# A hybrid encoder step on one core: a fixed order for the first loads and products, and regrouped outputs of state space and sample attention

## The chip, the core and the metric

The kernel runs on one core of a Trainium2 chip. The metric is device microseconds of one execution. Before the change the median of 3 runs is 2015.0 us (2014.14 to 2017.74). Engines are named as in the profile: PE is TensorE's products, PEld its weight loads, DVE VectorE, ACT ScalarE, POOL GpSimd, SP SyncE, which issues all DMAs of this kernel.

## The reference, cut to what matters

One layer works on a prompt of 1024 tokens and on 32 sample tokens with a past of 2048, all in float32, width 2048. The input is normalised, scaled and shifted by a modulation of the condition vector, and projected; four head groups read the projection, and a common output projection follows.

```python
shift, scale, gate = jnp.split(c @ w_mod + b_mod, 3, axis=-1)
u = layer_norm(x) * (1.0 + scale[:, None]) + shift[:, None]
(z_a, xbc_a, dt_a, q_b, k_b, v_b, g_b, x_c, ...) = split_cols(u @ w_in)
# A, state space, per chunk with carried state h:
y = jnp.einsum('bthn,bshn,btsh,bshp->bthp', cc, bc, decay, xdt)
y = y + jnp.einsum('bthn,bhpn,bth->bthp', cc, h, jnp.exp(acum))
# B, stick-breaking attention, swept over key blocks:
z = jnp.einsum('bqhd,bkhd->bhqk', qblk, k) * scale
out = jnp.einsum('bhqk,bkhd->bqhd', w, v)
```

## The kernel before, in words

The prompt is worked in two halves (h = 0 and 1, 512 tokens each); the 32 sample tokens ride with half 0, so that a row of that half has 544 columns. A column tile is 128 columns of w_in: `col_tile` (L336) loads its two halves of 512 KB, splits each into a high and a low part (ScalarE cast L326, VectorE subtraction L327), and adds three products for each of the 16 blocks k of 128 rows (wh*uh, wh*ul, wl*uh, L351 to L353), in half 0 over two spans of 272 columns: 96 products. The normalised and scaled input u is kept in the same two parts, `uh` and `ul`. The scale is applied when u is built (`build_u0`, L280: five transposes, two ScalarE activations, two VectorE instructions). The shift stands in two extra columns of u (`shift_columns`, L275), which the tiles with `shift` multiply along; the four gate tiles T_G do without.

The modulation comes from `mod_group(g, part)` (L205), for four groups of 512 columns and two parts (1 is the scale, 0 the shift): 16 loads of 256 KB each, and four times a quad of products, 32 columns of weights each on four strips of the array; then the sum is copied out (L227), turned with four small products (L229) and added to scale or shift. At the start the program traces the loads and norms of x (L1358), then the four groups of part 1 with the builds of u between them (L1361 to L1365), then the four gate tiles woven with part 0 (L1436).

The order of instructions on each engine is not that of the program: a planner places them by priority (`high_priority`) and by when it takes them to be ready. `behind(a, b)` (L197) puts one instruction behind another on its engine. Buffers come from pools: `io` has 20, of which five hold parts of x until u is built; `wr` has 2, `wh` and `wl` 3 each; the PSUM pool `ip` has 3, `z` 2, `s` 2, `a` 1.

The state-space unit `a_unit` (L528) runs 5 chunks (4 in half 1) for each of two groups of four heads. `weights` (L556) prepares a chunk; its matrix L has an exponential on ScalarE (L584) and a product with the mask on POOL (L585). `outputs` (L589), one step later, multiplies L with x*dt for each head (L597), C with the state (L600), combines both on VectorE (L605, L607), and updates the state (L609 to L614). `turn` (L621), another step later, transposes the result (L624) and adds the skip term (L626). A float32 product is two records in the trace.

The sample attention `b_sample` (L871) takes two pairs of heads at a time. For each of five key blocks it makes the scores of four heads with two products against a weight tile that is zero outside its heads (L917, `qb` from L784 to L788), and the values with eight products of 128 weight columns and 64 moving columns (L896).

`weave` (L1408) interleaves units in given numbers of steps.

Of the kernel before, what the change touches and what calls it, by code (L numbers as in the profile page):

```python
# [62 lines left out]
def step_kernel(ctx, tc, xp, xs, cst, wmss, wmg, bgate, win, wsm, wout, lng, lnb, ck, cv,  # L63
# [140 lines left out]

    def mod_group(g, part):  # L205
        o = ZT("mod")

        for kq in range(4):
            ws = []
            for i in range(4):  # L210
                wr = IO("wmr")
                nc.sync.dma_start(wr[:, 0:512], wmss[g, 4 * kq + i, part])
                ws.append(wr)
                if i < 3:
                    yield 1

            with tc.high_priority():
                after = None
                for i in (3, 0, 1, 2):
                    c0 = 2 * (4 * kq + i)  # L220
                    mm = T.matmul(o[32 * i:32 * i + 32], cpad[:, c0:c0 + 32], ws[i][:, 0:512], start=(kq == 0),  # L221
                                  stop=(kq == 3), skip_group_check=True)
                    after = behind(mm, after)
            yield 1
        pc = ST("modc")
        mr = WK("mr")
        V.tensor_copy(mr[:, 0:512], o)  # L227
        for j in range(4):
            T.matmul(pc[:, 2 * j:2 * j + 2], mr[:, j * P:(j + 1) * P], sel2c, start=True, stop=True)  # L229
# [13 lines left out]
    def load_norm(src, rows, keep):  # L243

        tiles = []
        for q in range(4):
# [4 lines left out]
            nc.sync.dma_start(t[:rows, 0:512], src[:, q * 512:(q + 1) * 512])  # L251
# [28 lines left out]
    def build_u0(xts, k):  # L280
# [5 lines left out]
        for t in range(4):  # L286
            T.transpose(pt[:, t * P:(t + 1) * P], xts[t][0][q][:, o * P:(o + 1) * P], ident)
        pt2 = AT("xt2")
        T.transpose(pt2[:, 0:SMP], xts[4][0][q][0:SMP, o * P:(o + 1) * P], ident[0:SMP, 0:SMP])
# [3 lines left out]
        V.tensor_tensor(ul[:, 2:546], uf[:, 0:544], uh[:, 2:546].bitcast(F32), op=ALU.subtract)  # L293
# [90 lines left out]
    def narrow(h):  # L384
# [95 lines left out]
        for c in range(nch):  # L480
# [11 lines left out]
            A.activation(col[0:n, c, 24:32], col[0:n, c, 0:8], AF.Exp)  # L492
# [35 lines left out]
    def a_unit(h, g):  # L528
# [27 lines left out]
        def weights(c, n, cc):  # L556
# [30 lines left out]
            return L, xd, bt, el  # L587

        def outputs(c, n, cc, L, xd, bt, el):  # L589
# [11 lines left out]
            y = WK("ya", [P, 2, 256])  # L601
            if first:
                V.tensor_copy(y[0:n, 0, :], py[0:n, 0:256])
            else:
                V.tensor_tensor(g4(y[0:n, 1, :], 4), g4(py[0:n, 256:512], 4),  # L605
                                col[0:n, c, 24 + 4 * g:28 + 4 * g].to_broadcast([n, 4, 64]), op=ALU.mult)
                V.tensor_tensor(y[0:n, 0, :], y[0:n, 1, :], py[0:n, 0:256], op=ALU.add)  # L607
# [11 lines left out]
            return y  # L619

        def turn(n, cc, y):  # L621
            pt = ST("pyt")
            for j in range(2):
                T.transpose(pt[:, j * P:j * P + n], y[0:n, 0, j * P:(j + 1) * P], ident[0:n, 0:n])  # L624
            for j in range(2):
                V.scalar_tensor_tensor(yg[j][:, cc], tiles[f"x{j}"][:, cc], C("dsk", 2 * g + j),  # L626
                                       pt[:, j * P:j * P + n], op0=ALU.mult, op1=ALU.add)

        todo1 = todo2 = None
        for c in range(nch + 2):  # L630
            done = todo2
            todo2 = None
            if todo1:
                todo2 = (*todo1[1:3], outputs(*todo1))
                todo1 = None
            if c < nch:
# [3 lines left out]
                todo1 = (c, n, cc, *weights(c, n, cc))  # L640
            if done:
                turn(*done)
# [91 lines left out]
    def b_gate(p):  # L734

        res = yield from col_tile(0, T_G + p, False)
        t = WK("graw")
# [4 lines left out]
        yield 2  # L742

    def b_unit(h, p):
# [26 lines left out]
        if h == 0:  # L771
# [8 lines left out]

# [3 lines left out]
            qb = sp.tile([P, P], F32, tag="qb", name=nm("qb"), bufs=2)  # L784
            G.memset(qb, 0.0)
            o = (p % 2) * 64
            G.tensor_copy(qb[0:64, o:o + 32], q[0:64, 512:544])
            G.tensor_copy(qb[64:128, o + 32:o + 64], q[64:128, 512:544])  # L788
# [82 lines left out]
    def b_sample(gq):  # L871
# [13 lines left out]
        def back(blk, w, vc):  # L885
# [7 lines left out]
            for b in range(nb):  # L893
                for j in range(2):
                    lhs = prs[j][2] if blk == 4 else vc[j][:, b * P:(b + 1) * P]
                    T.matmul(pa[:, 64 * j:64 * j + 64], lhs, wt[0:kn, b * P + 64 * j:b * P + 64 * j + 64],  # L896
                             start=(blk == 4 and j == 0), stop=(blk == 0 and b == nb - 1), skip_group_check=True)

        todo = None
        for blk in (4, 3, 2, 1, 0):  # L900
# [14 lines left out]
            for j in range(2):  # L915
                rhs = prs[j][1] if blk == 4 else kc[j][:, 0:512]
                T.matmul(z[:, 0:n], prs[j][0], rhs, start=(j == 0), stop=(j == 1))  # L917
# [6 lines left out]
        for j in range(2):  # L924
            ys = sp.tile([P, SMP], F32, tag="ysb", name=nm("ysb"))
            for hh in range(2):
                r = slice(64 * hh, 64 * hh + 64)
# [635 lines left out]
```

## Time and profile before

| | |
|---|---|
| median of 3 runs | 2015.0 us (2014.14 to 2017.74) |
| profiled execution | 2011.09 us, span 2009.2 us, clock 0.989 |
| TensorE busy | 1916.5 us, 95% |
| VectorE busy | 1341.6 us, 67% |
| ScalarE busy | 767.0 us, 38% |
| GpSimd busy | 272.7 us, 14% |
| HBM read, written | 253.49 MB, 35.82 MB |

The span is the time from the first to the last instruction of the profiled execution. Busy times are records laid over each other; matmuls overlap, so the pace of TensorE is read from one start to the next.

### The profile page before, as it was taken

The page shows a single profiled execution, that of the slowest core. Times are in us where ns is not written, and L with a number is a line of the kernel's source. Part 1 is how long each engine was busy: PE and PEld are TensorE (multiplying, and loading weights), DVE is VectorE, ACT ScalarE, POOL GpSimd, SP SyncE. Part 2 cuts the span into 40 slices and gives each one's busy share as a digit, 9 for nine tenths or more (in the row PEclk, how much of TensorE's full clock was granted, in tenths as well). Part 3 has the DMA queues.
Part 4 walks back from the last instruction along what each step waited for, and adds up shares of the span by engine and source line. Part 5 has one row for each costly group of instructions (what it writes and reads, how often), then busy time and mean ns, then how long its engine had stood idle before and what let it go on. Part 6 is the DMA issues. An engine that isn't in the chain of part 4 may idle for free. (4 is left out here: it accounts for less than half of the span.)

```text
span 2009.2 us, 31503 instructions
## 1 busy us (share of the span) xinstructions
PE 1916.5 (95%) x11956; PEld 1599.0 (80%) x11956; DVE 1341.6 (67%) x2610; ACT 767.0 (38%) x1278; POOL 272.7 (14%) x481
## 2 busy tenths in 40 slices
PE   3999999999999999999999999999999999998998
PEld 1578999998889999977787886777878676676787
DVE  4325667877956857876678779876857664355765
ACT  5212533334464434435444444533334421133321
POOL 1000111202211202331101011121111210000000
PEclk9999999999999999999999999999999999999998
DMA  9786344333443343644232332433433635457733
GB/s 320 260 282 226 119 127 127 118 121 121 138 145 119 105 117 101 175 126 139 91 113 94 113 101 85 122 99 102 126 99 101 210 107 184 151 190 239 226 128 131
DMA packets 162031, 291.38 MB, mean 145 GB/s; under 512 B 23836, under 2 KB 66076, under 8 KB 161880
## 3 DMA queue, kind: packets, MB, share of 16 engines
q1 hardware_dynamic: 161880, 289.37, 45.3%
q8 instruction: 94, 1.54, 0.3%
q14 instruction: 57, 0.47, 0.1%
HBM read 253.49 MB, written 35.82 MB: 144 GB/s over the span
## 5 line engine op out<-in xcount | busy, mean ns | idle before, releaser
L351 PE MATMUL ip<-uh,wh 128*128 128x272 f32 (+4 forms) x2368 | 775.8, 328 | 0.4 <-POOL uh L277 0.4
L352 PE MATMUL ip<-ul,wh 128*128 128x272 f32 (+4 forms) x2368 | 765.6, 323 | 0.0
L353 PE MATMUL ip<-uh,wl 128*128 128x272 f32 (+4 forms) x2368 | 764.1, 323 | 0.0
L326 ACT CAST wh<-wr 128x1024 fp32r<-128x1024 f32 (+1 forms) x257 | 268.3, 1044 | 671.2 <-PE ip L352 404.8
L327 DVE TENSOR_TENSOR wl<-wr,wh 128x1024 fp32r<-128x1024 f32 (+1 forms) x257 | 314.6, 1225 | 253.8 <-ACT wh L326 239.4
L351 PEld LDWEIGHTS ip<-uh,wh 128*128 128x128 f32 x2368 | 449.5, 190 | 38.9 <-issue 7.7
L352 PEld LDWEIGHTS ip<-ul,wh 128*128 128x128 f32 x2368 | 449.4, 190 | 37.7 <-issue 7.0
L353 PEld LDWEIGHTS ip<-uh,wl 128*128 128x128 f32 x2368 | 449.3, 190 | 37.7 <-issue 7.3
L1241 PE MATMUL op<-wh,yh 128*128 128x512 f32 (+1 forms) x576 | 215.9, 375 | 7.6 <-DVE val L1252 7.6
L1243 PE MATMUL op<-wh,yl 128*128 128x512 f32 (+1 forms) x576 | 215.4, 375 | 0.0
L1242 PE MATMUL op<-wl,yh 128*128 128x512 f32 (+1 forms) x576 | 214.4, 372 | 0.0
L1103 DVE SCALAR_TENSOR_TENSOR cv<-cin,cs,cv 128x574 f32<-128x574 f32 (+1 forms) x240 | 187.4, 781 | 2.9
L1241 PEld LDWEIGHTS op<-wh,yh 128*128 128x128 f32 x576 | 109.0, 189 | 31.7 <-DVE val L1252 8.6
L1243 PEld LDWEIGHTS op<-wh,yl 128*128 128x128 f32 x576 | 109.0, 189 | 26.4 <-issue 7.3
L1242 PEld LDWEIGHTS op<-wl,yh 128*128 128x128 f32 x576 | 108.8, 189 | 22.3 <-issue 3.0
L1156 DVE SCALAR_TENSOR_TENSOR gacc<-wg,cs,gacc 128x512 f32<-128x512 f32 x120 | 89.1, 760 | 17.1 <-DMA wg<-in_wmg_dram 17.0
L804 POOL TENSOR_SCALAR_AFFINE_SELECT s<-s 128x128 f32<-128x128 f32 x64 | 35.4, 553 | 430.1 <-ACT s L702 429.8
L221 PE MATMUL mod<-wmr,cpad 128*32 128x512 f32 x256 | 38.2, 674 | 34.0 <-DMA wmr<-in_wmss_dram 34.0
L711 DVE TENSOR_TENSOR_SCAN pr<-kp 128x128 f32<-128x128 f32 (+4 forms) x66 | 54.0, 819 | 14.3 <-POOL kp L806 11.6
L702 ACT ACTIVATE s<-z 128x512 f32<-128x512 f32 (+3 forms) x96 | 47.7, 497 | 34.9 <-PE z L732 33.1
L715 DVE TENSOR_TENSOR s<-s,pr 128x512 f32<-128x512 f32 (+5 forms) x106 | 59.5, 564 | 2.0
L514 DVE SCALAR_TENSOR_TENSOR cv<-cin,cs,cv 128x547 f32<-128x547 f32 (+1 forms) x72 | 55.2, 767 | 0.3
(374 smaller groups left out, 2224.8 us busy)
## 6 DMA issues: line engine op xcount, KB each, us to landing
wr<-in_win_dram SPq DMA_DIRECT2D x192, 512.0 KB
wmr<-in_wmss_dram SPq DMA_DIRECT2D x128, 256.0 KB
wr<-in_wout_dram SPq DMA_DIRECT2D x63, 512.0 KB
wg<-in_wmg_dram SPq DMA_DIRECT2D x64, 256.0 KB
x<-in_xp_dram SPq DMA_DIRECT2D x32, 256.0 KB
out_dram<-val SPq DMA_DIRECT2D x32, 256.0 KB
xr<-in_xp_dram SPq DMA_DIRECT2D x28, 256.0 KB
yf<-ysc SPq DMA_DIRECT2D x16, 272.0 KB
```

The lines of the kernel that those rows point to most:

```text
L326: A.copy(wh, wr)
L327: V.tensor_tensor(wl, wr, wh.bitcast(F32), op=ALU.subtract)
L351: T.matmul(pt[:, 0:n], wh[:, k % 8, :], uh[:, c0:c0 + n], start=(k == 0), stop=False)
L352: T.matmul(pt[:, 0:n], wh[:, k % 8, :], ul[:, c0:c0 + n], start=False, stop=False)
L353: T.matmul(pt[:, 0:n], wl[:, k % 8, :], uh[:, c0:c0 + n], start=False, stop=(k == KD - 1))
L514: V.scalar_tensor_tensor(acc[:, 0:n], t[:, i:i + n], C(wname, j * tap + i), acc[:, 0:n], op0=ALU.mult, op1=ALU.add)
L715: V.tensor_tensor(s[0:rows, 0:m], s[0:rows, 0:m], pr[0:rows, 1:m + 1], op=ALU.mult)
L1103: V.scalar_tensor_tensor(acc[:, 0:n], t[:, i:i + n], C("cdw", 31 * j + i), acc[:, 0:n], op0=ALU.mult, op1=ALU.add)
L1156: V.scalar_tensor_tensor(acc[j][:, 0:512], wr[:, 0:512], cT[:, k, j:j + 1], acc[j][:, 0:512], op0=ALU.mult, op1=ALU.add)
L1241: T.matmul(acc[t][:, 0:w], yh[:, c], wh, start=(first and i == 0), stop=False)
L1242: T.matmul(acc[t][:, 0:w], yh[:, c], wl, start=False, stop=False)
L1243: T.matmul(acc[t][:, 0:w], yl[:, c], wh, start=False, stop=(last and i == len(ws) - 1))
```

## The change

The start becomes one function, `startup`, in which the DMAs of x, of the part 1 modulation and of the first w_in halves, the modulation products, their turns, the transposes of u and the products of two gate tiles are each put behind what was traced before them on their engine (`keep_in_program_order`). The two gate tiles are summed in four k groups as u comes, in four PSUM buffers at once. What is traced later on SP, POOL and VectorE is queued behind the last of those instructions (`issue_after`). The other two gate tiles stay with `b_gate`, woven with part 0.

```diff
+    def mod_sum(o, kq, ws):
+        for i in (3, 0, 1, 2):
+            c0 = 2 * (4 * kq + i)
+            yield T.matmul(o[32 * i:32 * i + 32], cpad[:, c0:c0 + 32], ws[i][:, 0:512], start=(kq == 0),
+                           stop=(kq == 3), skip_group_check=True)
...
-            nc.sync.dma_start(t[:rows, 0:512], src[:, q * 512:(q + 1) * 512])
+            d = nc.sync.dma_start(t[:rows, 0:512], src[:, q * 512:(q + 1) * 512])
+            if keep:
+                inorder(d)
...
-        V.tensor_tensor(ul[:, 2:546], uf[:, 0:544], uh[:, 2:546].bitcast(F32), op=ALU.subtract)
+        return (G.tensor_tensor(ul[:, 514:546], uf[:, 512:544], uh[:, 514:546].bitcast(F32), op=ALU.subtract),
+                V.tensor_tensor(ul[:, 2:514], uf[:, 0:512], uh[:, 2:514].bitcast(F32), op=ALU.subtract))
...
+        def quads(g):
+            ws = []
+            for kk in range(KD):
+                wr = IO("wmr")
+                begun[0] = inorder(nc.sync.dma_start(wr[:, 0:512], wmss[g, kk, 1]))
+                ws.append(wr)
+            if g < 2:
+                load_weights(0, g)
+                load_weights(1, g)
+            o = ZT("mod")
+            for kq in range(4):
+                for mm in mod_sum(o, kq, ws[4 * kq:4 * kq + 4]):
+                    inorder(mm)
+                yield o
+        def part(x, g):
+            for i, (c0, t0, _, n) in enumerate(sp_):
+                for k in range(4 * g, 4 * g + 4):
...
+                    inorder(T.matmul(o, wh, uh[:, c0:c0 + n], start=(k == 0), stop=False))
+                    inorder(T.matmul(o, wh, ul[:, c0:c0 + n], start=False, stop=False))
+                    inorder(T.matmul(o, wl, uh[:, c0:c0 + n], start=False, stop=(k == KD - 1)))
+        for o in quads(0):
+            pass
+        for g in range(4):
+            mod_columns(g, 1, o, inorder)
+            m = quads(g + 1) if g < 3 else iter(())
+            build_u0(xts, 4 * g)
+            build_u0(xts, 4 * g + 1)
+            o = next(m, None)
+            build_u0(xts, 4 * g + 2)
+            begun[1:] = build_u0(xts, 4 * g + 3)
+            next(m, None)
+            part(0, g)
+            next(m, None)
+            part(1, g)
+            next(m, None)
```

In the state-space outputs the result is made already turned, two heads beside each other on 64 array columns each; the state's share is added in PSUM, with a copy of C that is scaled by exp(acum) (`ce`). The outputs of a chunk are traced behind the weights of the next one; `turn` and the combining on VectorE go, and so does the small exponential in `narrow` (L492).

```diff
+            ce = WK("ce", [P, 4, P])
+            A.activation(ce[:, :, 0:n], bca[:, :, 0:n], AF.Exp)
+            G.tensor_tensor(ce[:, :, 0:n], ce[:, :, 0:n], tiles["C"][:, None, cc].to_broadcast([P, 4, n]), op=ALU.mult)
...
-            for hh in range(4):
-                T.matmul(py[0:n, hh * 64:(hh + 1) * 64], L[0:n, hh, 0:n], xd[0:n, 0, hh * 64:(hh + 1) * 64],
-                         start=True, stop=True)
-            if not first:
-                T.matmul(py[0:n, 256:512], tiles["C"][:, cc], Hc, start=True, stop=True)
+            for j in range(2):
+                for st in range(1 if first else 2):
+                    for i in range(2):
+                        hh = 2 * j + i
+                        hc = slice(hh * 64, (hh + 1) * 64)
+                        if st == 0:
+                            x, m = xd[0:n, 0, hc], L[0:n, hh, 0:n]
+                        else:
+                            x, m = Hc[:, hc], ce[:, hh, 0:n]
+                        T.matmul(py[64 * i:64 * i + 64, j * P:j * P + n], x, m, start=st == 0, stop=first or st == 1,
+                                 skip_group_check=True)
```

In the sample attention the query tile is no longer padded with zeros: each head's 64 rows and 32 columns are a product of their own. The values are made with the attention weights as the stationary side, 32 columns of each head on a strip of its own, and transposed once at the end.

```diff
-                for j in range(2):
-                    lhs = prs[j][2] if blk == 4 else vc[j][:, b * P:(b + 1) * P]
-                    T.matmul(pa[:, 64 * j:64 * j + 64], lhs, wt[0:kn, b * P + 64 * j:b * P + 64 * j + 64],
-                             start=(blk == 4 and j == 0), stop=(blk == 0 and b == nb - 1), skip_group_check=True)
+                for x in range(4):
+                    v = prs[x // 2][2] if blk == 4 else vc[x // 2][:, b * P:(b + 1) * P]
+                    T.matmul(pa[32 * x:32 * x + 32, 0:64], wt[0:kn, b * P + 32 * x:b * P + 32 * x + 32],
+                             v[0:kn, 64 * (x % 2):64 * (x % 2) + 64], start=blk == 4, stop=blk == 0 and b == nb - 1,
+                             skip_group_check=True)
...
-            for j in range(2):
-                rhs = prs[j][1] if blk == 4 else kc[j][:, 0:512]
-                T.matmul(z[:, 0:n], prs[j][0], rhs, start=(j == 0), stop=(j == 1))
+            for x in (2, 3, 0, 1):
+                j, r = x // 2, slice(64 * (x % 2), 64 * (x % 2) + 64)
+                rhs = prs[j][1][r, :] if blk == 4 else kc[j][r, 0:512]
+                after = behind(T.matmul(z[32 * x:32 * x + 32, 0:n], prs[j][0][r, :], rhs,
+                                        start=True, stop=True, skip_group_check=True), after)
```

The weaving numbers of the state-space units change with their steps (7 - h to 6 - h, and 9 - h to 8 - h).

## Rows read from the trace of the kernel before

**Rows 1.** Part 1 of the page: busy time of the engines.

```profile
PE 1916.5 (95%) x11956; PEld 1599.0 (80%) x11956; DVE 1341.6 (67%) x2610; ACT 767.0 (38%) x1278; POOL 272.7 (14%) x481
```

**Rows 2.** Windows: stretch, its length, each engine's busy time, clock, DMA.

```profile
core 0: us, PE busy (x) PEld busy (x) DVE busy (x) ACT busy (x) POOL busy (x), PEclk, DMA share, GB/s
0.00:30.00 30.00, 0.00 (x0) 0.00 (x0) 18.29 (x44) 16.35 (x23) 5.15 (x29) 1.00 0.88 288
30.00:40.00 10.00, 6.85 (x33) 0.97 (x33) 0.99 (x4) 5.33 (x9) 0.00 (x0) 1.00 1.03 379
200.00:1800.00 1600.00, 1564.51 (x9828) 1320.20 (x9828) 1130.46 (x2224) 653.94 (x1107) 256.96 (x412) 1.00 0.40 124
```

**Rows 3.** Timeline of PE at the start: start, duration, operation, idle before.

```profile
30.34 1.94 PE L221 MATMUL mod<-wmr,cpad 128*32 128x512 f32 x8 [30.34 <-DMA wmr<-in_wmss_dram]
...
39.08 1.06 PE L221 MATMUL mod<-wmr,cpad 128*32 128x512 f32 x8 [0.74 <-DMA wmr<-in_wmss_dram]
...
41.13 1.47 PE L229 MATMUL modc<-sel2c,mr 128*128 128x2 f32 x8 [0.98 <-DVE mr L227]
...
189.74 0.30 PE L351 MATMUL ip<-uh,wh 128*128 128x272 f32 x1
...
190.51 0.29 PE L409 MATMUL ipn<-uh,wb 128*128 128x274 f32 x1
```

**Rows 4.** Timeline of PE around one group of attention values (L843).

```profile
1020.52 0.28 PE L353 MATMUL ip<-uh,wl 128*128 128x256 f32 x1
1020.73 1.09 PE L843 MATMUL av<-wt,prev 128*64 128x128 f32 x16
1021.75 0.50 PE L351 MATMUL ip<-uh,wh 128*128 128x512 f32 x1
1022.10 0.40 PE L352 MATMUL ip<-ul,wh 128*128 128x512 f32 x1
1022.33 0.40 PE L353 MATMUL ip<-uh,wl 128*128 128x512 f32 x1
```

**Rows 5.** Timeline of PE at the last modulation quad.

```profile
164.72 1.06 PE L221 MATMUL mod<-wmr,cpad 128*32 128x512 f32 x8 [0.78 <-DMA wmr<-in_wmss_dram]
...
166.71 1.02 PE L229 MATMUL modc<-sel2c,mr 128*128 128x2 f32 x8
167.59 0.37 PE L352 MATMUL ip<-ul,wh 128*128 128x274 f32 x1
```

**Rows 6.** Timeline of PE at one state-space chunk.

```profile
786.25 1.00 PE L597 MATMUL py<-xd,L 128*128 128x64 f32 x8
787.08 0.65 PE L600 MATMUL py<-hst,cv 128*128 128x256 f32 x2
787.57 0.59 PE L609 MATMUL pst<-xd,bt 128*128 128x256 f32 x2
788.00 0.27 PE L566 MATMUL px<-ident,cv 128*128 128x128 f32 x1
788.11 0.27 PE L567 MATMUL px<-ident,cv 128*128 128x128 f32 x1
```

**Rows 7.** Tile uf: nanoseconds min/median/max, first and last start, forms.

```profile
L291 ACT ACTIVATE uf<-xt,scale x32: 279/486/690, 42.8 to 93.8; 128x32 f32<-128x32 f32 x16, 128x512 f32<-128x512 f32 x16
L293 DVE TENSOR_TENSOR ul<-uf,uh x16: 719/726/728, 44.8 to 94.6; 128x544 fp32r<-128x544 f32 x16
```

**Rows 8.** Tile L, and what line 597 waits for.

```profile
L584 ACT ACTIVATE L<-L x18: 310/632/634, 762.7 to 1619.2; 128x512 f32<-128x512 f32 x16, 32x128 f32<-32x128 f32 x2
L585 POOL TENSOR_TENSOR L<-L,gt x18: 446/1274/1596, 763.4 to 1619.9; 128x512 f32<-128x512 f32 x16, 32x128 f32<-32x128 f32 x2
...
  POOL L L585: 9.9, 14
```

**Rows 9.** Timeline of PE at a block of the sample attention.

```profile
533.60 1.88 PE L917 MATMUL zs<-kc,qb 128*128 128x512 f32 x4
535.32 0.60 PE L890 MATMUL wts<-ident,s 128*128 128x128 f32 x4
...
537.23 2.00 PE L896 MATMUL avs<-wts,vc 128*128 128x64 f32 x16
539.04 0.38 PE L353 MATMUL ip<-uh,wl 128*128 128x272 f32 x1
```

**Rows 10.** Timeline of PE at prompt scores: two heads on two row halves.

```profile
244.93 0.35 PE L731 MATMUL z<-kl,qh 64*128 64x384 f32 x2
245.11 0.34 PE L732 MATMUL z<-kh,ql 64*128 64x384 f32 x2
```

More of the change, by code (lines that the diff above doesn't have):

```diff
@@ L218, in mod_group, with mod_columns @@
                 after = None
[L219 to L222, printed above, removed]
+                for mm in mod_sum(o, kq, ws):
                     after = behind(mm, after)
             yield 1
+        mod_columns(g, part, o, lambda i: i)
+    def mod_columns(g, part, o, pin):
         pc = ST("modc")
@@ L595, in outputs @@
             py = ZT("py")
-            for hh in range(4):
-                T.matmul(py[0:n, hh * 64:(hh + 1) * 64], L[0:n, hh, 0:n], xd[0:n, 0, hh * 64:(hh + 1) * 64],
-                         start=True, stop=True)
-            if not first:
-                T.matmul(py[0:n, 256:512], tiles["C"][:, cc], Hc, start=True, stop=True)
[L601 to L607, printed above, removed]
+            for j in range(2):
[9 more added lines that the diff above has]
+                                 skip_group_check=True)
+            for j in range(2):
+                V.scalar_tensor_tensor(yg[j][:, cc], tiles[f"x{j}"][:, cc], C("dsk", 2 * g + j),
+                                       py[:, j * P:j * P + n], op0=ALU.mult, op1=ALU.add)
             pst = ST("pst")
@@ L618, in outputs @@
                 nc.sync.dma_start(o_ssmp[:, g * 256:(g + 1) * 256], Hc)
-            return y
-        def turn(n, cc, y):
-            pt = ST("pyt")
-            for j in range(2):
-                T.transpose(pt[:, j * P:j * P + n], y[0:n, 0, j * P:(j + 1) * P], ident[0:n, 0:n])
-            for j in range(2):
[L626 to L635, printed above, removed]
+        todo = None
+        for c in range(nch + 1):
+            done, todo = todo, None
             if c < nch:
@@ L639, in a_unit @@
                 cc = slice(c0, c0 + n)
-                todo1 = (c, n, cc, *weights(c, n, cc))
+                todo = (c, n, cc, *weights(c, n, cc))
             if done:
-                turn(*done)
+                outputs(*done)
             yield 1
@@ L914, in b_sample @@
             z = ZT("zs")
-            for j in range(2):
-                rhs = prs[j][1] if blk == 4 else kc[j][:, 0:512]
-                T.matmul(z[:, 0:n], prs[j][0], rhs, start=(j == 0), stop=(j == 1))
+            after = None
+            for x in (2, 3, 0, 1):
[3 more added lines that the diff above has]
+                                        start=True, stop=True, skip_group_check=True), after)
             w, carry = stick(z[:, 0:n], P, n, diag if blk == 4 else None, carry)
@@ L923, in b_sample @@
         back(*todo)
[L924 to L927, printed above, removed]
-                V.tensor_copy(ys[r], pa[r, 64 * j + 32 * hh:64 * j + 32 * hh + 32])
-            nc.sync.dma_start(ysc[0][4 + 2 * gq + j, :, 512:544], ys)
+        ys = sp.tile([P, 64], F32, tag="ysb", name=nm("ysb"), bufs=1)
+        V.tensor_copy(ys, pa[:, 0:64])
+        pt = ST("yst")
+        T.transpose(pt[0:64, 0:P], ys, ident)
+        yt = sp.tile([64, P], F32, tag="ysc", name=nm("ysc"), bufs=1)
+        V.tensor_copy(yt, pt[0:64, 0:P])
+        for x in range(4):
+            nc.sync.dma_start(ysc[0][4 + 2 * gq + x // 2, 64 * (x % 2):64 * (x % 2) + 64, 512:544],
+                              yt[:, 32 * x:32 * x + 32])
     def c_unit(h, hd):
@@ L1367, in small_states @@
+    startup()
+    for i in begun:
+        ctx.enter_context(tc.issue_after(i.ins))
+    sts1 = []
     def small_states():
@@ L1435, in step_kernel @@
         if h == 0:
[L1436 removed]
+            weave([(stage1(b_gate(p)), 2) for p in range(2, 4)], [(chain(*[mod_group(g, 0) for g in range(4)]), 64)])
         units = {"A": (Au, 12), "B": (B, 6 if h == 0 else 8), "C": (Cu, 4), "D": (Du, 4),
                  "G": ([d_gate(h, i) for i in range(4)], 2)}
[L1439 removed]
+        follow = {"A": (Au, 6 - h), "B": (B, 6 + 4 * h), "C": (Cu, 9 - 2 * h), "D": (Du, 11),
                   "d": ([d_finish(h)], 8)}
```

67 lines of the change are left out of this document (44 added, 23 removed).

## The prediction

> **What bounds the kernel now.** I read part 1 of the page first, then the windows of the start and of the middle, then the timeline of the start, and last the lines that the diff touches. TensorE is busy for 95% of the span [rows 1], and from 200 to 1800 us for 1564.5 of 1600 us [rows 2]: there a product that is taken away shortens the kernel by the time to the next product's start, unless its place is filled by a wait. (A record's own duration runs into the next one's, so I count start to start.) The start is different. TensorE does nothing until 30.34 us, and what it waits for is a DMA, the first modulation weights [rows 3]. By 30 us the DMAs have moved 30 x 288 = 8.64 MB and after that 379 GB/s [rows 2]. In that order came the x blocks (4.46 MB), constants (0.22 MB) and five half tiles of w_in (2.62 MB), all ahead of the first quarter group of modulation weights (1.05 MB), 8.35 MB together: the w_in tiles hold up the first product.
>
> **Part 1, the start.** I take two events that both kernels have. The first is the end of the first group's 16 modulation products: 39.08 + 1.06 = 40.14 us. The second is the end of the seventh column tile (four gates and q, k, v), where the narrow tile starts: 190.51 us [rows 3]. Between them 150.4 us pass. The work in it, at full pace:
> - 7 tiles x 96 products at (190.51 - 189.74) / 6 = 0.128 us [rows 3]: 86.0 us
> - 28 quads of modulation products (8 records) at 1.06 us [rows 3] and some 0.1 us for the change of tile shape (0.35 us instead of 0.23 for the product behind such a group [rows 4]): 32.5 us
> - 8 column turns (L229) at 167.59 - 166.71 = 0.88 us [rows 5]: 7.0 us
> - 80 transposes for u at 788.11 - 788.00 = 0.11 us [rows 6], and 16 x 0.1 us for changes: 10.4 us
>
> That is 135.9 us, so 14.5 us are waits and half pace.
>
> After the change the SP queue brings constants, x, the 16 weights of group 0 and only then w_in: 4.46 + 0.22 + 4.19 = 8.87 MB. By the windows 8.64 MB are there at 30 us, so this is there at 30.6 us. The last quad then runs at the cold pace, 1.94 us like the first one of before [rows 3], and the first event falls at 32.5 us instead of 40.1: 7.6 us won.
>
> The waits of the fixed order: behind each group's products TensorE stands until the sum is copied out, 41.13 - 40.14 = 1.0 us [rows 3]; before, other work can lie there, now the next pinned instruction is the turn itself: 4 us. Four builds of u take ScalarE about 1 us each (an estimate from the two activations of a build, 0.69 and 0.28 us [rows 7]) and TensorE 0.65 us; two quads lie between them, so some 0.7 us a group stay: 3 us. The first turn and builds run cold, 1.47 us [rows 3] instead of 0.88 for the turn, 2 us in all. The modulation loads of the second half (part 0) come no faster than before, and the two gates left are shorter cover than four: 4 us. Sum 13 us against 14.5.
>
> Is the DMA fast enough between? A group needs 4.19 MB, the first two 5.24 MB with their w_in halves: 13 to 16 us at 0.32 to 0.38 MB/us. TensorE needs for a group 48 x 0.128 + 4 x 1.16 + 0.88 + 2.6 + the waits = 16 us. They are level, with a lead of 11 to 15 buffers, so I add nothing. The start gives -7.6 - 1.5 = **-9 us**; bounds -18 (no new waits) and +8 (TensorE waits a third longer for each group). All later SP, POOL and VectorE work is queued behind the start; SP's last pinned load goes out when group 3's buffers come free, and behind it wait the gate and part 0 loads, which is the 4 us above.
>
> The split of the low part of u (32 columns to POOL) takes some 0.04 us from VectorE's 0.73 us [rows 7] and hides under the builds; POOL has nothing else there.
>
> **Part 2, state-space outputs.** Per chunk these go: 8 records of py (787.08 - 786.25 = 0.83 us), the product with the state (0.49 us) and two transposes (0.22 us): 1.54 us [rows 6]. In their place come 16 records with 64-column weights and 128 moving columns, two heads beside each other. The attention values (L843) have just this shape: 1.02 us for 16, and 0.12 + 0.09 us for the change of shape on both sides [rows 4]: 1.22 us. So -0.3 us for each of 18 chunks (the first chunk of a group has no state product; it loses and gains less): -5.5 us; bounds -9 (no cost of the shape) and +3 (pairs run one behind the other, 0.107 us a record as in py).
>
> VectorE loses 2 x 0.41 us a chunk, which was off the path. New are an exponential on ScalarE (0.63 us [rows 8]) and a product on POOL, 1.27 us like the one that is there [rows 8], behind it in POOL's order; the py group needs both. TensorE now waits 9.9 us in all, 14 times, for that first POOL product [rows 8]. The outputs of a chunk are now traced behind the next chunk's weights, which hides most: +2 us, bounds 0 and +10. Together **-3.5 us**.
>
> **Part 3, sample attention.** Scores: two products of 128 x 512, 535.32 - 533.60 = 1.72 us [rows 9], become four of 64 rows and 32 columns that lie in different rows and columns of the array. The modulation quad (four column strips, 512 columns) takes 1.06 us [rows 3], with the change 1.2 us: -0.5 us x 8 blocks = -4 us. Values: 16 records at 539.04 - 537.23 = 1.81 us [rows 9] become 32 with half the work in each strip. No row has 64 columns on four strips; scaled from the quad it is 0.5 us, at the pace of L843 (0.064 us a record) 2.05 us, each with 0.2 us for the change. I take 0.045 us a record, 1.64 us: -1.4 us, bounds -9 and +3. The transposes and DMAs at the end are two pairs and hide. Together **-5.5 us**.
>
> The nine small exponentials taken from the narrow stage lie beside products on ScalarE: nothing.
>
> **Sum.** -9 - 3.5 - 5.5 = -18 us. The profiled execution has 2009.2 us of span and 1.9 us around it, 2011.1 us, 0.2% under the median of 2015.0; -18 gives 1993 for it, and from the median **1997 us**.
>
> **Rivals.**
> - *Row halves that share a PSUM bank take turns* (0.10). The four score products of a block write one bank; halves of the array's rows alternate. If these cannot overlap, 8 records of 0.43 us make 3.4 us, +1.7 us a block in place of -0.5: 2015 - 18 + 17.6 = 2015 us, no change. For it: no row of before shows two row halves on one bank. Against it: two row halves that write two banks overlap here, 384 columns twice in 0.18 us [rows 10], where one alone needs 0.16. The Trainium skill (TensorEngine Tiling, Restrictions and Gotchas, Gotcha 1) says that different row tiles cannot access the same PSUM bank at once; by it the change would end at this rival's time. No run here shows it yet, and the partitions written differ.
> - *The fixed order keeps TensorE at the half clock* (0.14). Waits between short pieces could leave the first 60 us at 1.2 GHz, as the first quad shows with 1.94 instead of 1.06 us [rows 3]. From 32.5 us to the end of the two gates lie 192 x 0.128 + 12 x 1.16 + 3.5 + 10.4 = 52 us of work; run at half pace it costs 52 more. It decides from 18 us on, so with 35% of that work at half pace; with 60% it is 2015 - 18 + 31 = 2028 us. Against it: the fourth quad of before has the full pace although it waited 0.74 us for its data [rows 3].
> - *The start gives nothing* (0.05), because the part 0 loads end no earlier and q waits for its shift columns: 2015 - 9 = 2006 us. Before, the last of these products starts at 164.72 us, behind a wait of 0.78 us for its load [rows 5].
> - *All covers hold* (0.12): start -15, outputs -6, samples -11: 1983 us.
>
> **How the numbers follow.** The forecast has 0.59. Faster by over 0.2% (under 2011; what measurement of this kernel can tell): 0.58 + 0.12 + 0.05 = 0.75; within 0.2%: 0.10 and a remainder of 0.01: 0.11; slower: 0.14. The range runs from 1981 (just beyond the case in which all covers hold) to 2017, takes in the bank rival and leaves out the half clock.
>
> **What would show it.** First modulation product at about 21 us and the first group's end near 32; the narrow tile's start near 181 us; a granted clock of 1.0 from 45 us on; 16 records of py in about 1.0 us, and TensorE's waits for POOL in the outputs under 12 us; score groups of 8 records in 1.1 and not 3.4 us. I am wrong if the first group ends at 32 and the narrow tile still starts after 188, or if TensorE's idle time grows by what its work loses.

## The result and the profile after

The changed kernel took 1990.81 us (median of 4 runs, 1989.37 to 1994.12) against 2014.86 us before: ratio 0.988, 95% interval 0.9863 to 0.9897. On a second chip, beside some of the experiments, it was 0.9861 (0.9842 to 0.9881). It is faster by 24 us where 18 were forecast, and 1990.8 lies in the range. The span of the profiled execution fell from 2009.2 to 1987.6 us.

Part 1 of the page of the changed kernel, and the windows that answer to [rows 1, 2]:

```profile
PE 1901.5 (96%) x12194; PEld 1578.5 (79%) x12194; DVE 1338.2 (67%) x2573; ACT 773.8 (39%) x1288; POOL 301.2 (15%) x505
```

```profile
0.00:30.00 30.00, 6.81 (x32) 0.79 (x32) 14.93 (x39) 18.33 (x28) 3.70 (x24) 1.00 0.94 325
30.00:40.00 10.00, 9.04 (x45) 5.12 (x45) 6.63 (x11) 5.35 (x10) 2.25 (x3) 0.66 1.05 405
200.00:1800.00 1600.00, 1563.52 (x10127) 1311.85 (x10126) 1141.48 (x2219) 665.57 (x1124) 275.54 (x423) 0.99 0.40 127
```

From 200 to 1800 us TensorE is as full as before (1563.5 of 1600 us, before 1564.5): what was taken away there did not come back as waits. The timeline of the start, in answer to [rows 3]:

```profile
21.27 1.94 PE L213 MATMUL mod<-wmr,cpad 128*32 128x512 f32 x8 [21.27 <-DMA wmr<-in_wmss_dram]
...
28.92 1.06 PE L213 MATMUL mod<-wmr,cpad 128*32 128x512 f32 x8 [0.70 <-DMA wmr<-in_wmss_dram]
30.96 1.40 PE L238 MATMUL modc<-sel2c,mr 128*128 128x2 f32 x8 [0.98 <-DVE mr L236]
...
184.67 0.29 PE L421 MATMUL ipn<-uh,wb 128*128 128x274 f32 x1
```

The first group ends at 28.92 + 1.06 = 29.98 us, 10.2 us earlier; the narrow tile starts 5.8 us earlier. The next three are timelines of one sample block's scores, one block's values and one chunk of the state-space outputs [rows 9, 6]:

```profile
526.64 1.06 PE L928 MATMUL zs<-kc,qb 64*32 64x512 f32 x8
527.63 0.66 PE L896 MATMUL wts<-ident,s 128*128 128x128 f32 x4
...
549.80 0.65 PE L903 MATMUL avs<-vc,wts 128*32 128x64 f32 x32
550.38 0.39 PE L365 MATMUL ip<-uh,wl 128*128 128x272 f32 x1
...
774.51 0.44 PE L623 MATMUL py<-L,xd 128*64 128x128 f32 x4
...
775.54 0.70 PE L629 MATMUL pst<-xd,bt 128*128 128x256 f32 x2
```

Start to start, the scores of a block take 0.99 us (before 1.72), its values 0.58 us (before 1.81), and the 16 records of py 1.03 us.

Where the time went I read from the start of the same column-tile product (the lines of ip, counted from 0) in each trace. Besides the start there are two stages: the one with the sample attention (products 2304 to 3456) and the rest of the column tiles (3456 to 7103), in which the outputs lie. In brackets is what the granted clock took: length of a 10 us window x (1 - its clock), summed over the stage.

```
us                     narrow starts   2304 to 3456   3456 to 7103
before                 190.51          221.9 (0.0)    899.4 (5.1)
after                  184.67          208.7 (1.7)    896.8 (8.5)
after, second run      185.69          209.0 (1.7)    890.9 (1.7)
start alone            185.59          224.1 (1.7)    900.7 (5.1)
samples alone          193.01          210.0 (1.7)    898.8 (3.4)
outputs alone          188.87          222.3 (1.7)    897.7 (8.5)
scores alone           189.31          219.5 (3.4)    901.5 (3.4)
```

So of the 21.5 us by which the last column-tile product is earlier, 5.8 are the start, 13.2 the samples and 2.6 the outputs (5 to 6 with the clock's part set aside). The four executions with the old start reach the narrow tile at 188.9 to 193.0 us, the six with the new one at 184.7 to 188.6: means 190.4 and 186.3, so the start is worth 4 to 6 us there.

### The profile page after: what moved, and what is told of

It is laid out like the page before. It is cut to its first block, busy times and chain, and to the rows that moved or that the text cites. A ratio compares the mean times of both kernels' runs of the same rounds, so it can differ in the third digit from the quotient of the medians.

```text
span 1987.6 us, 31999 instructions
## 1 busy us (share of the span) xinstructions
PE 1901.5 (96%) x12194; PEld 1578.5 (79%) x12194; DVE 1338.2 (67%) x2573; ACT 773.8 (39%) x1288; POOL 301.2 (15%) x505
## 5 line engine op out<-in xcount | busy, mean ns | idle before, releaser
L363 PE MATMUL ip<-uh,wh 128*128 128x272 f32 (+3 forms) x2304 | 759.1, 330 | 0.7 <-POOL uh L288 0.7
L364 PE MATMUL ip<-ul,wh 128*128 128x272 f32 (+3 forms) x2304 | 747.4, 324 | 0.0
L365 PE MATMUL ip<-uh,wl 128*128 128x272 f32 (+3 forms) x2304 | 745.7, 324 | 0.0
L338 ACT CAST wh<-wr 128x1024 fp32r<-128x1024 f32 x253 | 264.0, 1044 | 635.3 <-PE ip L364 362.9
L339 DVE TENSOR_TENSOR wl<-wr,wh 128x1024 fp32r<-128x1024 f32 x253 | 312.1, 1235 | 240.1 <-ACT wh L338 222.5
L363 PEld LDWEIGHTS ip<-uh,wh 128*128 128x128 f32 x2304 | 438.7, 190 | 42.0 <-issue 9.6
L365 PEld LDWEIGHTS ip<-uh,wl 128*128 128x128 f32 x2304 | 438.2, 190 | 35.7 <-issue 4.5
L364 PEld LDWEIGHTS ip<-ul,wh 128*128 128x128 f32 x2304 | 438.2, 190 | 32.9 <-issue 4.3
L1072 POOL TENSOR_TENSOR dn<-dn,mhalf 128x1 f32<-128x1 f32 (+1 forms) x36 | 27.8, 771 | 211.6 <-DVE dn L1071 207.9
```

Of the source, the lines that this page charges most:

```text
L338: A.copy(wh, wr)
L339: V.tensor_tensor(wl, wr, wh.bitcast(F32), op=ALU.subtract)
L363: T.matmul(pt[:, 0:n], wh[:, k % 8, :], uh[:, c0:c0 + n], start=(k == 0), stop=False)
L364: T.matmul(pt[:, 0:n], wh[:, k % 8, :], ul[:, c0:c0 + n], start=False, stop=False)
L365: T.matmul(pt[:, 0:n], wl[:, k % 8, :], uh[:, c0:c0 + n], start=False, stop=(k == KD - 1))
```

## The experiments

**Each part alone.** Three kernels, each the kernel before with one part of the change.

```diff
 # start alone: only the pinned start of the change
...
+    startup()
...
```

> The start alone: the kernel before with the fixed order of the first loads and products, outputs and samples as before. Theory (the parts are independent, the start is worth what the two traces show at the narrow tile, 190.51 against 184.67 us): 5 to 7 us faster than before, narrow tile at 184 to 186 us. Rival (the start's lead is given back later, and the whole gain is the samples' and the outputs' products): within 2 us of before.

Measured: 2012.62 us against 2018.31, ratio 0.9976 (0.996 to 0.9992), by the ratio 4.8 us faster (1.6 to 8.1), with the narrow tile at 185.59 us. That is close to the theory's 5 to 7 us, but the interval does not quite leave out the rival (within 2 us), and the one trace does not show the lead kept: its last column-tile product starts at 1571.9 us, that of the kernel before at 1571.7.

```diff
 # samples alone: the scores and the values
...
-                for j in range(2):
...
+                for x in range(4):
...
```

> The sample attention alone, scores and values regrouped, all else as before. Theory (products of four strips lie beside each other, 8 score records in 1.0 us and 32 value records in 0.6 us): 12 to 15 us faster than before, all of it between the first and the last sample block. The forecast of the prediction for this part was 5.5 us. Rival (a part of the trace's 13 us in that stretch is a new order of other work, which the start brought): 5 to 9 us.

Measured: ratio 0.9952 (0.9933 to 0.9971), 9.7 us faster (5.9 to 13.5). That is less than the theory's 12 us and more than the rival's 9, and the interval takes in both. Its trace has 11.9 us less in the sample stage, with the start as before, but a late narrow tile (193.01 us), which is no part of the edit.

```diff
 # outputs alone: two heads on 64 array columns each, ce in place of the state product's scaling
...
-                T.matmul(py[0:n, 256:512], tiles["C"][:, cc], Hc, start=True, stop=True)
...
+                        T.matmul(py[64 * i:64 * i + 64, j * P:j * P + n], x, m, start=st == 0, stop=first or st == 1,
+                                 skip_group_check=True)
...
```

> The state-space outputs alone, with their weaving numbers and without the small exponential of the narrow stage. Theory (1.0 us for 16 records with 64 columns in place of 1.5, less some waits for POOL): 2 to 5 us faster. Rival (the second POOL product of a chunk takes back what the products lose): no change, within 2 us, and TensorE's waits for POOL above the 9.9 us of before.

Measured: ratio 0.9978 (0.9964 to 0.9991), 4.4 us faster (1.8 to 7.3), as the theory had it; the wait that the rival asked to see above 9.9 us is 6.9 us in its view of tile L. The three add up to 18.9 us against 24, each uncertain by about 3 to 4 us: nothing shows that the parts need each other. By the traces the samples are the largest part (11.9 to 13.2 us against 4 to 6 of the start); the intervals of the times overlap.

**Scores or values?** The kernel before with the new scores and the old values:

```diff
...
-                T.matmul(z[:, 0:n], prs[j][0], rhs, start=(j == 0), stop=(j == 1))
...
+                after = behind(T.matmul(z[32 * x:32 * x + 32, 0:n], prs[j][0][r, :], rhs,
+                                        start=True, stop=True, skip_group_check=True), after)
```

> Only the scores of the sample attention regrouped, the values as before. Theory (row halves that write one bank overlap, 1.0 us a block in place of 1.72, eight blocks): 4 to 6 us faster than before, so that the values carry 8 to 10 of the samples' gain. Rival (halves take turns, and the score records of the changed kernel only look short): 10 us slower or more.

Measured: 2016.86 us, ratio 1.0004 (0.9987 to 1.0021). The bank rival falls: its price was 10 us or more, and the 8 score records take 0.99 us here as well, on one bank. But the gain of the scores, 4 to 6 us expected, is not seen in the time: the interval ends at 2.6 us faster. The trace shows part of the reason, in the rows of one block:

```profile
551.87 1.72 PE L915 MATMUL zs<-kc,qb 64*32 64x512 f32 x8 [1.25 <-DMA kc<-in_ck_dram]
553.52 1.11 PE L886 MATMUL wts<-ident,s 128*128 128x128 f32 x4
```

Behind a wait of 1.25 us for the keys the same group takes 1.65 us in place of 0.99 us, part of it at half clock (the window from 550 us has 0.83). A wait need not end so: in the kernel with the samples alone the same group waits 0.90 us for its keys and takes its short time. The stage is 2.4 us shorter, and 5.8 us with the 3.4 us of the clock set aside, which is 8 x (1.72 - 0.99). Whether the timed executions lost the rest in this way their times do not show, so how the samples' gain divides into scores and values is read from the rows and not from the times.

**Why the values are so short.** The changed kernel with the values' loop turned round, so that the 8 products of one strip follow each other:

```diff
-            for b in range(nb):
-                for x in range(4):
+            for x in range(4):
+                for b in range(nb):
```

> The changed kernel with one loop turned round: in the sample attention's values the 32 products of a block go strip by strip (8 behind one another on the same 32 array columns) in place of going round the four strips. Same products, same operands. Theory A: the values cost 0.018 us a record in the changed kernel only because four neighbours in the order lie on four strips and run beside each other; strip by strip each record waits for the one ahead, some 0.05 to 0.065 us a record, 1.6 to 2.0 us a block in place of 0.58 us, 8 to 11 us over the 8 blocks, so 0.4 to 0.55% slower than the changed kernel and the sample stage 9 us longer. Rival B: the products are short because each streams only 64 columns, and the order is nothing: 0.6 us a block and the same time within 2 us.

And two strips at a time, 16 products that alternate between the first two and then 16 between the others:

```diff
-            for b in range(nb):
-                for x in range(4):
+            for x, b in [(2 * a + x, b) for a in range(2) for b in range(nb) for x in range(2)]:
```

> The changed kernel with the values' 32 products of a block in another order: 16 that alternate between the first two strips, then 16 that alternate between the other two. Round the four strips a block took 0.58 us, strip by strip 1.40 us. If the pace is set by how many strips lie beside each other (theory A), two give about half of the single strip's time, 0.7 us plus the change, some 0.7 to 0.8 us a block, and the sample stage is 1 to 2 us longer than the changed kernel's. Rival B: there is a floor of one record each 0.018 us whatever the strips, which two strips reach as well: 0.58 us. Rival C: only four different neighbours overlap: 1.2 to 1.4 us.

The timelines of one block's values, strip by strip and then in pairs:

```profile
556.77 1.39 PE L902 MATMUL avs<-vc,wts 128*32 128x64 f32 x32
558.09 0.39 PE L365 MATMUL ip<-uh,wl 128*128 128x272 f32 x1
```

```profile
553.80 0.90 PE L902 MATMUL avs<-vc,wts 128*32 128x64 f32 x32
554.63 0.39 PE L365 MATMUL ip<-uh,wl 128*128 128x272 f32 x1
```

Written one strip at a time a block takes 1.32 us, two 0.83, four 0.58. Strip by strip the sample stage is 214.7 us, 6.0 longer than the changed kernel's, and 8 x (1.32 - 0.58) = 5.9; the time is 2001.1 us, ratio 0.9907 (0.9882 to 0.9932), 5 to 9 us more than the changed kernel's two ratios give. In pairs it is 212.3 us, 3.6 longer, of which 2.0 are the values and 0.8 a longer wait for the keys; this kernel ran once, at 1996.3 us. Theory A of both holds in direction: the pace is set by how many strips lie beside each other. Its size was too high for one strip (1.6 to 2.0 us expected). The records tell why, though they do not name their strip. In the changed kernel each round of four starts 0.056 us behind the last, and 32 such steps in a row would be 1.8 us, in theory A's range. But the first round takes 0.243 us a record there and the later ones 0.219, and by that mark a new strip begins every 0.254 us in the strip by strip kernel, before the one ahead is through its eight records. In the pair kernel the 11th and 12th records have the mark, 0.26 us behind the group's start: the second pair seems to begin when only 10 of the first pair's 16 have started, so that products on free strips start ahead of older ones on busy strips. This is read from durations, not shown by a name.

**The same question for the outputs.** The two products of one head behind each other, in place of alternating heads:

```diff
-                for st in range(1 if first else 2):
-                    for i in range(2):
+                for i in range(2):
+                    for st in range(1 if first else 2):
```

> The changed kernel with the state-space outputs in another order: the two products of one head (64 array columns) behind each other, then those of the head beside it, in place of alternating heads. Same products. Theory A (the outputs' group is short because neighbours lie on different halves of the columns): the 16 records of py take 1.4 to 1.7 us in place of 1.03 us, 7 to 12 us over 18 chunks, less what TensorE's wait for POOL in them hides, so 0.2 to 0.6% slower than the changed kernel. Rival B (the gain comes from the dropped transposes and state product alone): 1.0 to 1.1 us and no change.

```profile
780.12 0.45 PE L623 MATMUL py<-L,xd 128*64 128x128 f32 x4
780.39 0.40 PE L623 MATMUL py<-ce,hst 128*64 128x128 f32 x4
780.61 0.44 PE L623 MATMUL py<-L,xd 128*64 128x128 f32 x4
780.83 0.44 PE L623 MATMUL py<-ce,hst 128*64 128x128 f32 x4
781.19 0.70 PE L629 MATMUL pst<-xd,bt 128*128 128x256 f32 x2
```

The group takes 1.07 us, not 1.4 to 1.7: by that theory A falls, but the edit did not make what it was to make. It was to put the first head's products of ce ahead of the second head's of L, and the rows still show four records of L and then four of ce. The first ten records start in pairs some 13 ns apart (7 ns in the changed kernel). Whether the planner or TensorE brought them together no run separates. So that the outputs are short because halves overlap is not refuted, only not shown. The time was 1995.52 us, ratio 0.9899 (0.9875 to 0.9924), against 0.9861 (0.9842 to 0.9881): the intervals overlap, and 18 x 0.05 us would be 0.9 us. What the rest is stays open; between 800 and 1900 us its trace has five 10 us windows of clock 0.83 or lower, and the changed kernel's on the same chip three.

**What takes back the start's lead.** The changed kernel is 8.6 us ahead of the one before at the first column-tile product (39.9 us) and 8.9 us at the 384th (135.3 us), but 5.8 us from the 544th (168.4 us) on. First the loads of part 0, halved (the kernel leaves out one half of the shift's weights and uses the other half twice):

```diff
...
-                nc.sync.dma_start(wr[:, 0:512], wmss[g, 4 * kq + i, part])
+                nc.sync.dma_start(wr[:, 0:256], wmss[g, 4 * kq + i, part][:, 0:256])
...
```

> The changed kernel with half the bytes in the modulation loads of the second half (part 0, the shift): only 256 of 512 columns of each are loaded and used twice, so the shift isn't the reference's; number and shape of the products are unchanged. Theory A (these loads take the start's lead back): the last product group of part 0 starts 3 to 5 us before its 159.3 us of the changed kernel, the narrow tile at 180 to 182 in place of 184.67 us, and the kernel ends 2.5 to 5 us earlier. Rival B (the two gates left are too short a cover, or the order of the products does it): the narrow tile starts within 1 us of 184.67 and the time is the same within 2 us.

Measured: the last part 0 quad starts at 132.23 us (158.88 in the changed kernel; the expectations' 159.3 is the start of its last record), the narrow tile starts at 178.88 us, and the time is 1983.93 us, ratio 0.9832 (0.9809 to 0.9855). Theory A holds, beyond its size. Then the same bytes with more free buffers:

```diff
-                wr = IO("wmr")
+                wr = (WK if kk % 2 else IO)("wmr")
```

> The changed kernel with half of the pinned modulation weights of the first half (part 1) held in the other work pool, so that the loads behind them find more free buffers. Theory A (the loads' pace takes the lead back, and it is set by when buffers come free): the second half's loads go out earlier, the last part 0 products start 1 to 4 us before 159.3 us, the narrow tile 1 to 4 us before 184.67 us, and the kernel is 0.05 to 0.2% faster than the changed one. Rival B (the loads are limited by what the DMAs move): the narrow tile starts within 1 us of 184.67 us. Rival C (the other pool's buffers are wanted by the copies of the sums and of the gates): up to 3 us slower.

Measured: the last part 0 quad at 153.77 us and the narrow tile at 179.50 us, 5.2 us earlier, though the bytes are the same. The loads of part 0 in the changed kernel and in this one (the two times are the first issue and the last):

```profile
L222 SPq DMA_DIRECT2D wmr<-in_wmss_dram x64: 327/382/1387, 76.1 to 153.1; - x64
L222 SPq DMA_DIRECT2D wmr<-in_wmss_dram x64: 327/382/772, 65.8 to 148.4; - x64
```

So what held them is when the loads can go out, and not only what the DMAs move. How that makes 5.2 us is shown in part: TensorE's waits between the two events fall by 2.7 us, only 0.9 of it waits for these loads, the clock takes 1.7 us less, and the planner also placed the quads at other points between the column tiles. The time is 1988.62 us, ratio 0.9856 (0.9833 to 0.9879), which overlaps the changed kernel's: a gain at the end is not shown. Then the wait for the sum's copy, with 12 products put in front of it:

```diff
...
-            part(1, g)
-            next(m, None)
+            part(1, g, (0,))
+            next(m, None)
+            part(1, g, (1,))
...
```

> The changed kernel with the last quad of each group put one step earlier in the fixed order, ahead of the second row block of the second gate tile, so that 12 products lie between the group's last product and its column turn, where TensorE now stands 1.0 us for the sum's copy. Theory A (the waits of the order are real, but what paces the start behind 130 us is loads): at the 192nd product 1 to 3 us earlier than the changed kernel, at the narrow tile's start less than 1 us, the time the same within 2 us. Rival B (waits carry through): the narrow tile starts 2 to 3 us earlier, and the kernel ends 2 to 3 us earlier. Third: the group's last weights aren't there that early, TensorE waits for them and the gain is nothing at the 192nd product too.

In this kernel and in the changed one, the rows around the second group's turn (in that order):

```profile
46.58 1.06 PE L213 MATMUL mod<-wmr,cpad 128*32 128x512 f32 x8
...
49.19 0.95 PE L238 MATMUL modc<-sel2c,mr 128*128 128x2 f32 x8
...
52.29 1.07 PE L213 MATMUL mod<-wmr,cpad 128*32 128x512 f32 x8
```

```profile
47.35 1.06 PE L213 MATMUL mod<-wmr,cpad 128*32 128x512 f32 x8
49.31 1.05 PE L238 MATMUL modc<-sel2c,mr 128*128 128x2 f32 x8 [0.89 <-DVE mr L236]
52.32 1.94 PE L213 MATMUL mod<-wmr,cpad 128*32 128x512 f32 x8
```

Without the wait the next quad takes 1.07 us, with it 1.94 us: the wait is followed by half clock. This is no accident of one execution: in all eight profiled executions with the new start and this wait the quad behind the second turn takes 1.93 or 1.94 us, and in both with the wait covered (here and in the kernel with both edits) 1.07 us. From 50 to 90 us the changed kernel's windows, and those of the covered one behind them:

```profile
50.00:60.00 10.00, 9.45 (x60) 5.72 (x60) 6.13 (x12) 3.29 (x8) 2.99 (x4) 0.83 0.69 233
60.00:70.00 10.00, 8.96 (x68) 6.17 (x71) 1.48 (x4) 1.55 (x4) 0.13 (x1) 0.95 0.84 273
70.00:80.00 10.00, 9.80 (x66) 5.89 (x59) 3.84 (x7) 1.81 (x5) 2.86 (x4) 0.88 0.68 219
80.00:90.00 10.00, 9.04 (x58) 5.50 (x58) 2.62 (x6) 4.07 (x7) 0.88 (x2) 0.83 1.01 361
```

```profile
50.00:60.00 10.00, 9.09 (x66) 5.83 (x69) 6.83 (x12) 4.29 (x10) 2.86 (x4) 1.00 0.81 275
60.00:70.00 10.00, 9.71 (x75) 6.39 (x67) 3.09 (x6) 2.45 (x7) 1.49 (x2) 1.00 0.76 256
70.00:80.00 10.00, 9.90 (x76) 7.05 (x76) 2.92 (x5) 2.47 (x5) 1.50 (x2) 1.00 0.94 338
80.00:90.00 10.00, 9.42 (x69) 6.47 (x69) 7.38 (x16) 4.32 (x10) 3.10 (x7) 1.00 0.65 234
```

The column ahead of the last two is the granted clock: 5.1 us are lost to it in the first fence, none in the second. At the 192nd product the covered kernel is 5.4 us ahead of the changed one, more than every theory gave; at the narrow tile 2.8 us are left. From 90 us on it waits 3.2 us for part 0 loads, the changed kernel 2.0. Rival B has the number there, and theory A the mechanism of the loss. The time is 1988.99 us, ratio 0.9854 (0.9833 to 0.9876); it overlaps the changed kernel's and decides between neither.

**Both edits**, and the changed kernel beside them on the same chip:

> The changed kernel with both edits of the start that helped alone: the last quad of each group one step earlier (12 products cover the sum's copy) and half of the pinned modulation weights in the other work pool. Theory A (two separate losses, waits up to 150 us and late loads of the second half behind it): the narrow tile starts 6 to 9 us before the changed kernel's 184.67 us, where the two edits alone gave 2.8 and 5.2, and the kernel is 0.3 to 0.45% faster than the changed one. Rival B (the loads are the limit whatever the order): the narrow tile starts as with the buffers alone, 179 to 180 us, and the time is the buffers' one.

> The changed kernel itself once more, beside the next ones on this chip, so that they are compared with it and not with its runs on another one. Expected by every theory: the ratio of the first comparison, 0.988, within 0.002, and the narrow tile's start within 1.5 us of 184.67 us.

The repeated kernel fell where it was expected (0.9861, narrow tile at 185.69 us). The narrow tile of the two, changed kernel ahead, the one with both edits behind:

```profile
185.69 0.29 PE L421 MATMUL ipn<-uh,wb 128*128 128x274 f32 x1
```

```profile
177.48 0.29 PE L421 MATMUL ipn<-uh,wb 128*128 128x274 f32 x1
```

That is 8.2 us against the execution beside it, and 7.2 us against the first one (184.67), from which the two edits alone gave 2.8 and 5.2: theory A, two losses that add. The time is 1984.29 us against 1987.4, ratio to before 0.9828 (0.9804 to 0.9851): the lowest ratio of all, but its interval overlaps the changed kernel's, so that it is faster is shown at the narrow tile and not at the end.

## Why the prediction was right, and where not

**First event, -7.6 forecast, -10.2 measured.** The w_in tiles did hold up the first product: it starts at 21.27 us (forecast about 21). The last quad was not cold: it waited 0.70 us and took 1.06 us, where 1.94 was assumed. That part is luck of the execution: of the ten profiled executions with the new start four have this quad at 1.06 or 1.07 us and six at 1.85 to 1.94. The data was also there 1.7 us earlier, since the DMAs moved 325 GB/s to 30 us and not the 288 of before.

**Between the events, -1.5 forecast, +4.3 measured.** This step failed: the narrow tile starts at 184.67 us and not near 181. The stretch now takes 184.67 - 29.98 = 154.7 us, 18.8 beyond the 135.9 of work, where 13 were forecast. Before, the 14.5 us beyond the work were 6.9 us of waits, 5.1 us of granted clock and 2.5 us of neither; now they are 8.3, 8.5 and 2.0. The waits in that stretch and the windows of lower clock before:

```profile
PE modc L229 <- DVE mr L227: 3.7, 4, 1.0
PE mod L221 <- DMA wmr<-in_wmss_dram: 2.3, 4, 0.8
PE xt L287 <- ACT uf L291: 0.5, 3, 0.2
PE ip L351 <- POOL uh L277: 0.4, 1, 0.4
40.00:50.00 10.00, 9.02 (x47) 6.03 (x44) 4.38 (x9) 3.68 (x8) 0.00 (x0) 0.66 0.99 362
80.00:90.00 10.00, 8.94 (x67) 5.03 (x69) 1.88 (x4) 1.73 (x4) 0.00 (x0) 0.97 1.05 406
90.00:100.00 10.00, 10.00 (x68) 6.39 (x61) 4.79 (x8) 3.50 (x7) 0.00 (x0) 0.86 0.41 155
```

The waits in that stretch of the changed kernel:

```profile
PE modc L238 <- DVE mr L236: 4.7, 5, 1.0
PE mod L213 <- DMA wmr<-in_wmss_dram: 2.0, 2, 1.1
PE xt L300 <- ACT uf L302: 0.9, 4, 0.3
PE ip L363 <- POOL uh L288: 0.7, 1, 0.7
```

The last four are 8.3 us, less than the 11 forecast (4 + 3 + 4): the sums' copies cost what was said, but the wait on the builds is 0.9 and not 3 us. The mis-sized term is "cold, 2 us": the granted clock took 8.5 us, 3.4 in the window from 30 to 40 us and 5.1 from 50 to 90 (10.2 in the changed kernel's second execution). The forecast priced each 1.0 us wait at itself, and each of the first ones was followed by work at 1.2 GHz. The half-clock rival was thus right in kind and small in size: it spoke of 60% of the work to the end of the gates, and needed 18 us to decide. "A granted clock of 1.0 from 45 us on" was wrong. That part 0 loads pace the end was named (4 us); TensorE's waits for them are 2.0 us, and the kernel with more buffers shows that letting them out earlier is worth 5.2 us at the narrow tile. One figure of the overlap check is also off: 4.19 to 5.24 MB at 0.32 to 0.38 MB/us are 11 to 16 us and not 13 to 16, which changes nothing.

**Samples, -5.5 forecast, -13.2 measured in the trace and -9.7 alone.** Scores: 0.99 us, against 1.2, so 8 x 0.73 = 5.8 us in place of 4. Values: 0.018 us a record (0.58 / 32), where I took 0.045. No row had 64 columns on four strips, and I took a value between two ends, the pace of a row on two halves of the array and the 0.5 us scaled from the quad on four strips; the second end was the right one. 0.045 is near what one strip at a time costs (1.32 / 32 = 0.041). 8 x 1.23 = 9.8 us in place of 1.4; this term, just beyond its bound of -9, is by the rows why the kernel is faster than forecast. By these rows both together are 15.6 us; the stage shows 13.2, and the clock took 1.7 us more of it than before.

**Outputs, -3.5 forecast, -4.4 alone and -2.6 between the traces.** 16 records in 1.03 us (1.02 forecast). TensorE's waits did not rise: the view of tile L has 6.1 us for POOL (7 times), against 9.9 (14 times) [rows 8]. I misread that row: it adds the waits of the weight loads to those of the products, for the products alone it is 3.7 us before and 2.2 after. TensorE waits 0.4 us, once, for the new product on POOL; that tracing the outputs behind the next chunk's weights is what hides it was not run by itself.

**The bank rival** fell: scores on two row halves and one bank took 0.99 us, where taking turns asked for 3.4. The sentence of the Trainium skill that stands behind it (TensorEngine Tiling (Array Packing), Restrictions and Gotchas, Gotcha 1) does not hold for these products, which write different partitions of that bank. Another page of the Trainium skill (PSUM — Partial Sum Buffer, Terms), where it speaks of engines and not of row halves, says that different groups of 32 partitions of one bank may be accessed at the same time. These rows would agree with that for row halves too.

The sum: start -5.8 for -9, samples -13.2 for -5.5, outputs -2.6 for -3.5. The total was within the range because a low term and a high one partly cancelled; that part of it is luck.

## What to carry to other kernels

Small matrix products on column strips of their own are worth the most where they alternate over as many strips as there are: for 64 columns two strips took 0.63 of the time of one, and four 0.44. Price a wait on TensorE in a thin stretch at more than itself: look at whether the next products of known shape take their long or their short time, and put a dozen products between a result and the copy that TensorE needs back. When the work gets ahead of its loads, look at which buffers the loads wait for before the bandwidth is blamed.

## What the runs showed of the hardware

The half clock comes back late in the kernel too, and not in each execution. From 920 to 930 us the changed kernel's first profiled execution and its second one show this:

```profile
920.00:930.00 10.00, 10.00 (x29) 6.70 (x29) 3.82 (x20) 4.25 (x8) 0.00 (x0) 0.54 0.29 77
```

```profile
920.00:930.00 10.00, 8.03 (x40) 5.31 (x41) 6.31 (x30) 4.66 (x10) 0.00 (x0) 1.00 0.29 79
```

29 products in place of 40: the second execution is 2.6 us behind the first at the same product ahead of this window and 1.6 us ahead of it behind the window, 4.2 us in all. What TensorE did ahead of it differs too: in the window from 910 us it was busy for 7.52 us in the first execution and for 9.48 in the second. So two executions of one kernel differ by more than some of the edits above, which is why they are read stage by stage. And the clock's column reads 1.00 over the first 30 us, while the first quads take 1.94 us, and in the covered kernel still 1.00 where a quad at 35.38 us takes 1.94: up to its first fall the durations tell the pace and the column does not.

Products of different strips seem not to start in the order in which they were written (by the durations in the pair kernel's records). What is measured is that the written order of two products on a half decided little (1.07 us for 1.03), and that of 8 or 16 on a strip or two much (1.32 and 0.83 us for 0.58).
